# Two accumulator tiles for the last output strip of the first block's layers, and the squares of x on ScalarE

## The chip, the core and the metric

The kernel runs on one core of one Trainium2 chip. The core has TensorE (PE, with a weight load PEld ahead of each matmul), VectorE (DVE), ScalarE (ACT), GpSimd (POOL) and SyncE (SP), whose queue issues nearly all of the weight transfers here. The metric is the device time of one execution in microseconds (us).

## What is computed

A first block of two layers and a second block of one layer work on 256 tokens of width 2048. What matters here is how a layer of the first block ends and what follows it:

```python
# first block, layer l = 0, 1
mixed = jnp.concatenate([a_out, b_out, c_out], axis=-1)     # 256 x 2048
x = x + jnp.einsum('bsm,md->bsd', mixed, w_out[l])
# next layer, or the end of the block: x * rsqrt(mean(x*x) + EPS) * g
# second block
mod = silu(c) @ w_ada + b_ada          # six rows of 2048, and two more from w_ada_final
h = rms_norm(x, g_mix) * (1 + sc1) + sh1
...                                    # two attentions, output projection, residual
h = rms_norm(x, g_ffn) * (1 + sc2) + sh2
y = hier_moe(h)                        # router, then 32 experts
```

All of it is float32; a product with a weight is made of three matmuls on high and low parts.

## The kernel before

**Projections.** `proj` loads a weight strip of 512 columns in chunks of four blocks of 128 rows (`q`, 1 MB each, line 133). Each chunk is split in two halves (`hf`) into a high and a low part: ScalarE casts (L266), VectorE subtracts (L267), into one of three buffers `hl`. A half gives 12 matmuls in the token-major form (L295): two row blocks, two token halves `tb`, three products. With `by_op` false the 12 follow their half. With `by_op=True` the last chunk, and with `by_op="all"` every chunk, waits for both halves and then does the 12 matmuls of token half 0 and after them the 12 of token half 1.

**Accumulators.** `accum()` takes one of two PSUM tiles (pool `pa`, each of two banks, one for each token half). `Halves` takes both: one tile for each token half. It stands in the kernel before too, for the last strip of the second block's second output projection.

**End of a layer.** `layer` runs `part` for output strips 0 to 3 and `fin` after each. `fin` adds each token half of the accumulator to `x` (L919) and sums its squares (L920, by `square`: ScalarE at L378, VectorE at L380). In layer 1 it also multiplies x by the final gain (L922), sums the squares once more (L923) and, after the last strip, a chain of small operations (L953 to L961) leads by a power on GpSimd to the factor that the second block's first matmuls need.

**The modulation rows and the credit.** The eight rows `mod` (order 1, 0, 2, 4, 3, 5, 7, 6) are not made on TensorE. `ada_gen` makes them on VectorE in 256 steps: each takes one 512 KB load `araw` (three buffers, issued on SP's queue, L554) and one multiply-add over 128x1024 (L572; the first two of a row are L570). After 32 steps four small products on TensorE (`adap`, L578) sum a row up, and only then is the one buffer `ada` free for the next row. The steps are strewn among other work by a credit: `tick()` adds 0.590 after each half of a chunk, and a whole credit emits one step. `proj` doesn't call `tick` for a chunk that goes by `by_op`. What has not been emitted when the second block's last output strip begins is emitted there at once, by `ada_finish()` ahead of that strip's `proj`.

**Order.** The program gives each operation its place by a list scheduler: it goes by the order in which the operations are emitted and fills gaps that it foresees with later ones; each engine and SP's queue then run their list in order. `high_priority` around `fin` moves its operations ahead.

After the second block's output projection come the router (L1253 and on, many small VectorE operations), the gather (L1384) and the experts, whose weights (`ew`) go into buffers as these come free, those of `araw`, `ada`, `raw` and `hl` among them.

Of the kernel before, what the change touches and what calls it, by code (L numbers as in the profile page):

```python
# [94 lines left out]
def tile_kernel(tc, a, out, dbg=None):  # L95
    nc = tc.nc
    es = ExitStack()
    V = nc.vector
    A = nc.scalar
# [27 lines left out]
    def uid(s):  # L127
        cnt[0] += 1
        return f"{s}{cnt[0]}"
# [150 lines left out]
    def nb_ops(c, m):  # L280

        return [("N", c, m, tb, 0, tb) for tb in range(2)]
# [15 lines left out]
    def accum(name=None):  # L298
        return pa.tile([P, 2, 512], F32, tag="acc", name=name or uid("acc"))
# [74 lines left out]
    def square(xs, acc, eng):  # L374

        j = wk.tile([P, 512], F32, tag="stage", bufs=3, name=uid("sq"))
        if eng is A:
            A.activation(j, xs, AF.Square, accum_out=acc)  # L378
        else:
            V.scalar_tensor_tensor(j, xs, 1.0, xs, op0=OP.mult, op1=OP.mult, accum_out=acc)  # L380
# [90 lines left out]
    def mtile(name):  # L471
        return big.tile([P, 2, 4, S], F32R, tag="xm", bufs=7, name=name)
# [4 lines left out]
    ssq = sm.tile([P, 2, 4], F32, tag="ssq", name="ssq0")  # L477
# [132 lines left out]
    def layer(l, xT, ssq):  # L610
        w_in = a["w_in"][l]
        mT = [mtile(uid("mT")) for _ in range(4)]
# [47 lines left out]
        acc = latent(3078, 4, False)  # L660
# [3 lines left out]
        acc, started = accum(), set()  # L664
# [120 lines left out]
        acc = proj(w_in, 1536, 512, xT, nb_ops(0, 512))  # L785
# [3 lines left out]
        acc = proj(w_in, 2048, 262, xT, nb_ops(0, 262))  # L789
# [49 lines left out]
        for g in range(2):  # L839
            t = pslot([P, 4, S], F32, uid("cqk"))  # L840
            acc = proj(w_in, 4678 + 512 * g, 512, xT, tb_ops(4))
# [5 lines left out]
        acc = proj(w_in, 5702, 512, xT, nb_ops(0, 512))  # L847
# [8 lines left out]
        acc = proj(w_in, 6214, 512, xT, nb_ops(0, 512))  # L856
# [10 lines left out]
        for h in range(4):  # L867
# [19 lines left out]
            ssq = small(2, uid("css"))  # L887
# [15 lines left out]
        ssq = sm.tile([P, 2, 4], F32, tag="ssq", name=uid("ssq"))  # L903
        nxT = []
        accs = {}
        started = {s: set() for s in range(4)}

        def part(s, qs):
            accs[s] = proj(a["w_out"][l], 512 * s, 512, mT, nb_ops(0, 512), qs=qs, acc=accs.get(s), started=started[s],
                           final=qs[-1] == 3, by_op=True)  # L910

        def fin(s):
            if l == 1:
                gf = wk.tile([P, 512], F32, tag="stage", bufs=3, name=uid("gf"))
                nc.sync.dma_start(gf, a["final_norm_g"][512 * s : 512 * s + 512].unsqueeze(0).to_broadcast([P, 512]))
            with tc.high_priority():
                for tb in range(2):
                    xs = x[:, tb, 512 * s : 512 * s + 512]
                    V.tensor_add(xs, accs[s][:, tb, :], xs)  # L919
                    square(xs, ssq[:, tb, s : s + 1], V if l == 1 and s == 3 and tb else A)  # L920
                    if l == 1:
                        V.tensor_mul(xs, xs, gf)  # L922
                        square(xs, ssq1[:, tb, s : s + 1], V if tb else A)  # L923
            if l == 0:
                nxT.append(transpose_strip(s, "norm_g", 16))
# [14 lines left out]
    for l in range(DEPTH):  # L940
        xT, ssq, ssq1 = layer(l, xT, ssq)
# [154 lines left out]
    for u in range(2):  # L1096
# [5 lines left out]
        acc = proj(w_in, 3584 + 512 * u, 512, hT, nb_ops(0, 512))  # L1102
# [7 lines left out]
    for gp in range(2):  # L1110
        mT2.append(mtile(uid("oT")))
        qa = projT(512 * gp, "qa", qsplit)
        if gp == 0:
            ka = pslot([P, 4, S], F32, "ka")
            va = ka[:, 2:4, :]
            acc = proj(w_in, 1024, 512, hT, tb_ops(2) + [("N", 256, 256, 1, 0, 0), ("N", 256, 256, 1, 256, 1)])
# [100 lines left out]
    for s in range(4):  # L1217
        if s == 3:
            ada_finish()
        add_half(s, proj(a["w_out_2"][0], 512 * s, 512, mT2, nb_ops(0, 512), qs=(0, 1), by_op="all" if s == 3 else False,  # L1220
                         acc=Halves() if s == 3 else None), ra)
# [316 lines left out]
    for c0, n in STRIPS:  # L1538
# [8 lines left out]
        for v in range(4):  # L1547
            s, o = (c0 + m * v) // 512, (c0 + m * v) % 512
            h = slice(CAP * v, CAP * v + CAP)
            V.tensor_mul(yv(i, s)[P - CAP : P, o : o + m], ps[h, :], gt2(s)[h, o : o + m])  # L1550
        for s in range(c0 // 512, (c0 + n) // 512):
            xs = [x[:, tb, 512 * s : 512 * s + 512] for tb in range(2)]
# [11 lines left out]
    for s in range(4):  # L1564
        c = slice(512 * s, 512 * s + 512)
        for tb in range(2):
            xs = x[:, tb, c]
# [32 lines left out]
```

## Time and profile before

| | us |
|---|---|
| median of 3 runs | 2367.68 |
| lowest, highest | 2366.15, 2375.21 |
| profiled execution, device time | 2365.31 |
| its span, first to last instruction | 2363.6 |

TensorE is busy for 89% of the span, VectorE for 53%, ScalarE for 34%. The page cuts the span into 40 slices of 59 us. In the first 23 TensorE is busy for 80% or more nearly everywhere; from about 1390 us on, the transfers of the expert weights fill the 16 DMA engines at about 420 GB/s. Rows of the timeline give start, duration, engine, line, operation, what is written and read, the count, and in brackets the idle time of the engine ahead of it with what ended it. Rows that the profiler merged cover several instructions.

### The profile page before, as it was taken

The numbers are of one execution on the slowest core, as the hardware profiler recorded it, in microseconds if no ns is written. First come the engines' busy times: TensorE is split into PE (matmuls) and PEld (weight loads), VectorE is DVE, ScalarE is ACT, GpSimd is POOL, SyncE is SP. The second block draws the span as 40 slices with busy tenths as digits, with TensorE's granted clock in tenths as the row PEclk, the third lists the DMA queues.
The fourth block names the chain that finished last, engine by engine and source line by source line (L and its number), as shares of the span: only waits on it lengthen the run. The fifth ranks groups of instructions, "written<-read, shape, count | busy, mean of one in ns | idle before, by whom it ended". The sixth has DMA issues, their size and how long they took to land.

```text
span 2363.6 us, 32559 instructions
## 1 busy us (share of the span) xinstructions
PE 2108.8 (89%) x12919; PEld 1507.8 (64%) x12919; DVE 1253.7 (53%) x1990; ACT 793.6 (34%) x1583; POOL 100.0 (4%) x149
## 2 busy tenths in 40 slices
PE   8999999999999999899999988878777869696975
PEld 8999997799899977798786774333232424241421
DVE  5787687787776877775866871103021212121323
ACT  5553545545535555545555421100000101010111
POOL 0000100000100000202001000000000000000000
PEclk9999999999999999999999989989888989998998
DMA  6688787686797986796856899999999999999996
GB/s 212 219 298 286 240 313 268 235 306 205 242 311 249 317 287 231 231 339 185 308 187 237 291 356 376 421 421 421 421 419 421 421 421 421 421 421 421 421 421 253
DMA packets 221032, 760.82 MB, mean 322 GB/s; under 512 B 22464, under 2 KB 43276, under 8 KB 172616
## 3 DMA queue, kind: packets, MB, share of 16 engines
q1 hardware_dynamic: 215720, 750.88, 84.0%
q0 software_dynamic: 4960, 7.71, 1.5%
q8 instruction: 103, 1.69, 0.3%
q14 instruction: 57, 0.47, 0.1%
q10 hardware_dynamic: 192, 0.08, 0.0%
HBM read 755.68 MB, written 2.97 MB: 321 GB/s over the span
## 4 chain that ended last, share of the span: by engine, by line
PE 54%; DMA 26%; issue 11%; DVE 7%; ACT 2%; POOL 0%; SPq 0%; DVEq 0%; POOLq 0%; ACTq 0%
PE acc L291 19%; PE acc L295 16%; DMA ew<-in_w_up_dram 13%; DMA ew<-in_w_down_dram 6%; PE xg L1384 5%; DMA araw<-in_w_ada_dram 4%; PE acc L1428 2%; DVE ada L572 2%; PE gu L1406 2%; DVE hl L267 2%; PE s L431 2%; DMA araw<-in_w_ada_final_dram 2%; PE guT L1414 1%; PE pT L460 1%; PE op L1032 1%
## 5 line engine op out<-in xcount | busy, mean ns | idle before, releaser
L266 ACT CAST hl<-raw 128x1024 fp32r<-128x1024 f32 (+4 forms) x478 | 423.9, 897 | 493.6 <-PE acc L291 250.4
L267 DVE TENSOR_TENSOR hl<-raw,hl 128x1024 fp32r<-128x1024 f32 (+4 forms) x478 | 488.4, 1034 | 151.3 <-ACT hl L266 150.6
L291 PE MATMUL acc<-xT,hl 128*128 128x256 f32 x3744 | 469.5, 285 | 6.3 <-DVE hl L267 3.3
L291 PEld LDWEIGHTS acc<-xT,hl 128*128 128x128 f32 x3744 | 455.8, 192 | 12.1 <-ACT hl L266 5.2
L572 DVE SCALAR_TENSOR_TENSOR ada<-araw,cact,ada 128x1024 f32<-128x1024 f32 x240 | 306.9, 1287 | 79.9 <-DMA araw<-in_w_ada_dram 60.8
L1406 PE MATMUL gu<-ew,xe 128*32 128x512 f32 x1528 | 241.9, 646 | 92.3 <-DMA ew<-in_w_up_dram 58.9
L1419 DVE SCALAR_TENSOR_TENSOR eth<-eth,guT 128x128 f32<-128x128 f32 x32 | 9.2, 288 | 440.6 <-ACT eth L1418 440.6
L1411 ACT COPY gus<-gu 128x512 f32<-128x512 f32 x32 | 18.8, 586 | 613.0 <-PE gu L1406 613.0
L1406 PEld LDWEIGHTS gu<-ew,xe 128*32 128x32 f32 x1528 | 51.9, 114 | 267.0 <-issue 101.0
L295 PE MATMUL acc<-hl,mT 128*128 128x512 f32 x768 | 188.2, 397 | 0.7 <-DVE hl L267 0.7
L1428 PE MATMUL acc<-ew,aT 128*32 128x512 f32 x992 | 157.2, 760 | 26.9 <-DVE aT L1421 22.2
L291 PE MATMUL acc<-hT,hl 128*128 128x256 f32 x1248 | 170.4, 291 | 3.6 <-DVE hl L267 3.6
L291 PEld LDWEIGHTS acc<-hT,hl 128*128 128x128 f32 x1248 | 157.6, 194 | 13.4 <-issue 9.3
L295 PEld LDWEIGHTS acc<-hl,mT 128*128 128x128 f32 x768 | 141.9, 189 | 33.2 <-issue 3.7
L295 PE MATMUL acc<-hl,xT 128*128 128x512 f32 (+1 forms) x768 | 155.5, 364 | 2.4 <-DVE hl L267 2.4
L295 PEld LDWEIGHTS acc<-hl,xT 128*128 128x128 f32 x768 | 131.3, 188 | 25.7 <-DVE hl L267 3.3
L1384 PEld LDWEIGHTS xg<-oh,xres 128*128 128x128 f32 x512 | 122.8, 328 | 36.7 <-issue 26.8
L1432 DVE TENSOR_TENSOR y<-acc,gt2A 32x512 f32<-32x512 f32 x93 | 63.6, 684 | 150.7 <-PE acc L1428 149.7
L1384 PE MATMUL xg<-oh,xres 128*128 128x128 f32 x512 | 131.4, 411 | 5.4 <-ACT C L1375 3.2
L1406 PE MATMUL gu<-ew,xet 128*32 128x512 f32 x504 | 89.2, 635 | 30.1 <-DMA ew<-in_w_up_dram 23.3
L295 PE MATMUL acc<-hl,oT 128*128 128x512 f32 x384 | 101.4, 412 | 0.2 <-DVE hl L267 0.2
L1428 PEld LDWEIGHTS acc<-ew,aT 128*32 128x32 f32 x992 | 31.5, 131 | 106.5 <-issue 60.5
(339 smaller groups left out, 2013.0 us busy)
## 6 DMA issues: line engine op xcount, KB each, us to landing
ew<-in_w_down_dram SPq DMA_DIRECT2D x128, 1024.0 KB, 19.8
ew<-in_w_up_dram SPq DMA_DIRECT2D x127, 1024.0 KB, 19.8
ew<-in_w_gate_dram SPq DMA_DIRECT2D x126, 1024.0 KB, 19.8
raw<-in_w_in_dram SPq DMA_DIRECT2D x124, 1024.0 KB, 6.8
araw<-in_w_ada_dram SPq DMA_DIRECT2D x192, 512.0 KB, 6.3
raw<-in_w_out_dram SPq DMA_DIRECT2D x48, 1024.0 KB, 6.4
araw<-in_w_ada_final_dram SPq DMA_DIRECT2D x64, 512.0 KB, 6.4
raw<-in_w_in_dram SPq DMA_DIRECT2D x16, 512.0 KB, 3.8
```

The source lines that it names most:

```text
L266: A.copy(dst_hi, src)
L267: V.tensor_sub(dst_lo, src, dst_hi)
L291: T.matmul(acc[:m, b, o : o + 256], w[:, u, c : c + m], xk[v], start=st, stop=last and j == 2, skip_group_check=True)
L295: T.matmul(acc[:, b, o : o + m], xk[v][:, P * tb : P * tb + P], w[:, u, c : c + m], start=st, stop=last and j == 2, skip_group_check=True)
L431: T.matmul(ps[:, c0 : c0 + n], q_(b), k_[:, 0:n], start=b + i == 0, stop=i == len(terms) - 1, skip_group_check=True)
L460: T.transpose(ps[:, P * i : P * i + P], t[:, P * i : P * i + P], ident)
L572: V.scalar_tensor_tensor(ah, raw, ck, ah, op0=OP.mult, op1=OP.add)
L1032: T.matmul(o[half, :S], vs[i][0], pTs[i][:, 0:256], start=True, stop=False, skip_group_check=True)
L1384: T.matmul(ps[:, m * j : m * j + m], quads(x[:, tb, :], k), oh[:, tb, :], start=j + tb == 0, stop=tb == 1, skip_group_check=True)
L1406: T.matmul(ps[c : c + CAP, :], xe(i, k + d)[:, CAP * b : CAP * b + CAP], gu(v, k + d), start=k == 0, stop=k == KT - 2, skip_group_check=True)
L1428: T.matmul(acc[CAP * s : CAP * s + CAP, 0, :], aT[:, f, :], wd(f, s), start=f == 0, stop=f == 3, skip_group_check=True)
L1432: V.tensor_mul(yv(i, s)[CAP * b : CAP * b + CAP, :], acc[h, 0, :], gt2(s)[h, :])
```

## The change

For strip 3 of both layers of the first block the accumulator is a `Halves`, and `by_op` is "all" in place of True. The square of x in layer 1, strip 3, token half 1 goes to ScalarE as the others do.

```diff
         def part(s, qs):
-            accs[s] = proj(a["w_out"][l], 512 * s, 512, mT, nb_ops(0, 512), qs=qs, acc=accs.get(s), started=started[s],
-                           final=qs[-1] == 3, by_op=True)
+            accs[s] = proj(a["w_out"][l], 512 * s, 512, mT, nb_ops(0, 512), qs=qs, acc=accs.get(s) or (Halves() if s == 3 else None),
+                           started=started[s], final=qs[-1] == 3, by_op="all" if s == 3 else True)
...
                     V.tensor_add(xs, accs[s][:, tb, :], xs)
-                    square(xs, ssq[:, tb, s : s + 1], V if l == 1 and s == 3 and tb else A)
+                    square(xs, ssq[:, tb, s : s + 1], A)
```

## Rows read from the trace of the kernel before

**Rows 1.** The page, 40 slices: busy tenths of TensorE and of the DMA engines.
```profile
PE   8999999999999999899999988878777869696975
DMA  6688787686797986796856899999999999999996
```
**Rows 2.** Chain of work that ended last, in time: start, us, what.
```profile
1381.01 5.98 DMA araw<-in_w_ada_final_dram
1387.08 1.28 DVE ada L572
1388.37 1.32 DVE u L1156 x2
...
1401.94 7.35 PE xg L1384 x32
```
**Rows 3.** Timeline of the end of layer 1, all engines.
```profile
947.81 1.28 DVE L919 TENSOR_TENSOR xres<-acc,xres 128x512 f32<-128x512 f32 x2
...
962.12 1.23 DVE L267 TENSOR_TENSOR hl<-raw,hl 128x1024 fp32r<-128x1024 f32 x1 [1.50 <-ACT hl L266]
...
969.19 1.04 ACT L266 CAST hl<-raw 128x1024 fp32r<-128x1024 f32 x1 [0.30 <-PE acc L295]
969.19 1.29 DVE L919 TENSOR_TENSOR xres<-acc,xres 128x512 f32<-128x512 f32 x2 [5.85 <-PE acc L295]
970.14 0.62 ACT L378 ACTIVATE sq<-xres 128x512 f32<-128x512 f32 x1
...
970.89 0.69 DVE L922 TENSOR_TENSOR xres<-xres,gf 128x512 f32<-128x512 f32 x1 [0.41 <-ACT sq L378]
...
973.02 0.69 DVE L380 SCALAR_TENSOR_TENSOR sq<-xres 128x512 f32<-128x512 f32 x1
...
974.09 0.16 DVE L958 SCALAR_TENSOR_TENSOR rr_t<-rr_s,rr_t 128x2 f32<-128x2 f32 x1
...
976.43 1.19 PE L366 MATMUL bc<-diag,ones 128*128 128x128 f32 x4 [7.28 <-DVE diag L365]
```
**Rows 4.** Timeline of TensorE at the end of layer 0.
```profile
493.39 1.95 PE L291 MATMUL acc<-xT,hl 128*128 128x256 f32 x15
```
**Rows 5.** Timeline of TensorE in the second block's last output strip.
```profile
1382.09 4.82 PE L295 MATMUL acc<-hl,oT 128*128 128x512 f32 x20
```
**Rows 6.** Line L572, the modulation steps: ns min/median/max, first and last start.
```profile
L572 DVE SCALAR_TENSOR_TENSOR ada<-araw,cact,ada x240: 1261/1280/2262, 110.9 to 1387.1; 128x1024 f32<-128x1024 f32 x120
```
**Rows 7.** Timeline of VectorE: the last modulation row's first steps and late ones.
```profile
1254.94 1.41 DVE L570 TENSOR_SCALAR ada<-araw,cact 128x1024 f32<-128x1024 f32 x2
...
1358.94 1.28 DVE L572 SCALAR_TENSOR_TENSOR ada<-araw,cact,ada 128x1024 f32<-128x1024 f32 x1
...
1366.33 3.67 DVE L572 SCALAR_TENSOR_TENSOR ada<-araw,cact,ada 128x1024 f32<-128x1024 f32 x3
...
1375.74 1.28 DVE L572 SCALAR_TENSOR_TENSOR ada<-araw,cact,ada 128x1024 f32<-128x1024 f32 x1
```
**Rows 8.** Stages: us, busy of PE, PEld, DVE, ACT, POOL (instructions), clock, DMA share, GB/s.
```profile
960.00:980.00 20.00, 12.28 (x55) 10.03 (x54) 11.47 (x24) 6.66 (x11) 5.59 (x8) 0.83 0.43 138
...
1280.00:1300.00 20.00, 20.00 (x83) 14.20 (x83) 15.48 (x32) 12.63 (x32) 1.47 (x2) 0.91 0.61 208
...
1360.00:1380.00 20.00, 20.00 (x109) 16.91 (x107) 19.05 (x27) 8.71 (x14) 0.00 (x0) 1.00 0.91 316
```
**Rows 9.** Timeline of SP's queue: issues of modulation and expert loads.
```profile
1377.05 4.29 SPq L554 DMA_DIRECT2D araw<-in_w_ada_final_dram  x3
...
1381.86 2.64 SPq L1173 DMA_DIRECT2D ew<-in_w_down_dram  x4
...
1411.20 0.33 SPq L1194 DMA_DIRECT2D ew<-in_w_up_dram  x1
```
**Rows 10.** DMA issues: queue, count, KB each, median us from issue to landing.
```profile
ew<-in_w_down_dram SPq DMA_DIRECT2D x128, 1024.0 KB, 19.8
...
araw<-in_w_ada_final_dram SPq DMA_DIRECT2D x64, 512.0 KB, 6.4
```

## The prediction

> **What bounds the kernel now.** I read the page's 40 slices first. Up to about 1390 us TensorE sets the pace; from there the expert weights keep the DMA engines full to the end [rows 1]. In that second part a delay is not won back: the loads stop when all buffers are full, and start again when the first expert's matmuls free them. So what counts is when TensorE finishes the first part, and what stands between its last product and the gather. I then read the timeline at the two places that the change touches, and the chain of waits and the queues at the end of the second block's output projection, because the change also moves credit there.
>
> At the end of layer 0 TensorE has no gap to win: it goes straight on with layer 1's first projection at 493.39 [rows 4]. At the end of layer 1 it waits. The last product ends at 969.16; both adds start behind it, at 969.19, although token half 0 was done 12 matmuls before. The chain of squares and gains runs until 974.25, the power and two small products follow, and TensorE has its next work at 976.43, after 7.28 us idle [rows 3]; the granted clock of this stage is 0.83 [rows 8].
>
> At the third place, the last modulation step stands on the chain that ended last: its load takes 5.98 us, the step starts at 1387.08, and the residual add of the last strip follows it at 1388.37 [rows 2]. That row has nothing to spare.
>
> **The change part by part.**
>
> *Two tiles, layer 1.* One strip is 96 matmuls; from the adds at 947.81 to those at 969.19 it takes 21.38 us, 0.223 us for each [rows 3]. Token half 0 is complete 12 x 0.223 = 2.67 us before the end, so its add (0.68), square, gain and second square fall beside token half 1's matmuls. Left behind the last product: one add, 969.19 to 969.87. The square on ScalarE waits for the cast that starts there at 969.19 and takes 1.04, so it starts at 970.23; from its start to the gain it took 970.89 - 970.14 = 0.75, giving 970.98; the gain 0.61 to the next start, giving 971.59; from the second square's start to the end of the small operations 974.25 - 973.02 = 1.23, giving 972.82. Against 974.25 that is **-1.4 us**. Without the cast in front it would be -1.8; if a further VectorE split (1.23 [rows 3]) lands in the chain, -0.2. TensorE's gap is still near 6 us, so I count nothing for the clock.
>
> *The square moved to ScalarE.* VectorE is rid of 0.69 [rows 3], but the gain overwrites x and must wait for the square. The sum above already has this wait; kept on VectorE, the step would have ended within 0.3 us of the same. It goes in at nothing of its own, bounds -0.7 to +0.8 (one such square either way).
>
> *Two tiles, layer 0.* Nothing to win [rows 4]: 0. Added waits: the two tiles are both there are. Token half 1's first matmul needs the tile of strip 2; its adds end 1.3 us behind strip 2's last product (947.81 to 949.09 [rows 3]), and 12 matmuls of token half 0, 2.67 us, stand ahead. The next projection needs tile 0, freed by the first add about 2 us before the strip ends. If one modulation step (1.28 [rows 6]) sits in front, both are still about even: 0, bound +1.3 for each of the four places.
>
> *Every chunk by token half.* A half's buffer is free after 18 of 24 matmuls, and the split into it is needed 12 matmuls, 2.67 us, later. The split costs 1.04 + 1.23 = 2.27 us [rows 3]. It fits by 0.4 us. The nearest rows are the same form in the second block: 20 matmuls in 4.82 us, 0.24 each, without a gap [rows 5]. I take +0.5 for the six chunk changes of both layers; ends 0 and +4 (half of them behind a step of 1.28).
>
> *The credit.* This is the part that the change does not name. With every chunk of strip 3 by token half, its 6 calls of `tick` go, in two layers 12 x 0.590 = 7.08 credits. Counting through the program, 246 steps are emitted before the flush at the second block's last strip, so 10 are flushed; after the change 238, so **18 are flushed**. In strip 3 itself the missing steps buy nothing, since TensorE has no gap there. All later row boundaries move too: the seventh row's sum, now emitted in the second to last attention projection, is emitted in the second block's first output strip; the eighth row, which now begins at 1254.94 [rows 7], can begin only behind it, some 5 to 27 us later.
>
> What do 8 more steps cost in the end? One step is 3.67 / 3 = 1.22 us of VectorE [rows 7]. From below: if they fill VectorE's idle time between 1280 and 1340 (4.5 of 20 us idle in the row shown [rows 8]), 0. From above: in the flush three buffers turn round in 9.4 us (1366.33 to 1375.74 [rows 7]), so 8 steps take 25 us if all stand ahead of the router. Between: VectorE is busy for 19.05 of 20 us in this stage [rows 8], so 8 steps are 9.8 us of work, of which some 2 us find idle time. I take **+8 us**: nearer to this row, since VectorE's small router operations can go into the steps' load waits, but a list in order also stalls when a load is later than its place foresaw.
>
> Moving the loads costs no bytes: 8 x 512 KB leave stages of layers 0 and 1 and come later, before the gather's release at about 1411 [rows 9]; they fill time in which the queue would otherwise stand still.
>
> **Sum.** -1.4 + 0 + 0.5 + 8 = **+7 us**. Made on the profiled execution it is 2365.3 + 7 = 2372.3; that execution lies 2.4 us below the median of the runs, which the change is measured against, so I put it at 2367.7 + 7 = 2374.7, rounded to **2374**.
>
> **The rivals.**
>
> *Rival 1, the steps catch up.* For it: with idle VectorE time from 1280 to 1340 a filling scheduler can bring 8 steps in. Against it: the eighth row starts later, and VectorE has least room just where the steps would pile up. Then only -1.4 and the 0.5 are left: 2366 to 2368.
>
> *Rival 2, the tail stalls the router.* The last loads are issued when their buffers come free, from about 1385 on, behind 4 MB of expert weights issued at 1381.86 on the same queue [rows 9]. Expert loads that stand in such a queue land after 19.8 us, modulation loads now after 6.4 [rows 10]; two rounds of three loads, each later by half of the difference or by all of it (6 to 13 us) and in VectorE's list ahead of router operations, make +12 to +26: 2380 to 2393. It decides once more than three steps are left when the last product ends.
>
> The Trainium skill, page "DMA: Bandwidth & Descriptors", section "Queues, rings and completion order", says that each DMA engine consumes the descriptors of a ring in order, and that SP has one ring on each engine. That speaks for rival 2: by it the loads behind those 4 MB wait for all of them. The landing times in the rows agree; no row shows a modulation load in that place.
>
> *Rival 3, the two tiles do nothing.* If the scheduler puts the first add behind the strip anyway, -1.4 falls away: 2376 with the rest as forecast.
>
> *Rival 4, a real gain.* More than 11.8 us would need most of a gap at every strip; the traces show 7.28 us in one place. 2354.
>
> **How the numbers follow.** 0.5%, 11.8 us, is about what a measurement of this kernel tells from no change: 2356 to 2379.5. The forecast (2369 to 2380) has 0.44, rival 1 0.20, rival 2 0.28, rival 3 0.05, rival 4 0.03. The forecast's upper edge and rival 2 beyond 2379.5 make slower 0.31, faster 0.03, same 0.66. The range runs from 2364, rival 1 with its best bound, to 2389, which leaves out rival 4 and the top of rival 2.
>
> **What would show it.** Right: at layer 1's end the first add starts about 2.7 us before the last product ends, and TensorE's idle time is near 6 us; fewer L572 steps in both strips 3; the eighth row's first step later than 1254.94; L572 steps behind 1388, among router operations, and a gather later than 1401.94. If the last step stays at about 1388, rival 1 is right; if router operations wait over 5 us on an `araw` load, rival 2. The prediction is wrong if TensorE shows gaps inside the two strips, or if the time falls by more than 2 us.

## The result and the profile after

| | kernel before | kernel after |
|---|---|---|
| median, us (four runs each) | 2366.91 | 2397.05 |
| lowest, highest | 2362.5, 2375.21 | 2387.26, 2401.64 |
| profiled execution, device time | 2365.31 | 2387.26 |
| its span | 2363.6 | 2385.6 |

The ratio of after to before is 1.0123, 95% interval 1.0100 to 1.0146: slower by 1.2%, some 30 us. The forecast was 2374 with a range up to 2389. The loss has the sign of the forecast and four times its size. The profiled execution of after is its fastest run, 22 us above that of before, so its trace shows about three quarters of the loss of the medians. One of the six runs of e8 below took 8565 us and is left out of its median and ratio.

The page's slices for TensorE and the DMA engines stand against [rows 1]:

```profile
PE   8999999999999999899899968969677968686985
DMA  6688796796696986796865888999999999999996
```

A slice is 59.6 us here. TensorE's 20th (1133 to 1193 us) has 8 in place of 9 and its 24th (1372 to 1431 us) 6 in place of 8; behind that the DMA engines are as full as they were. A slice is coarse: a stall of 15 us in the 22nd and 23rd doesn't show.

The end of layer 1, timeline of all engines (start, us, engine, line), against [rows 3]:

```profile
962.45 0.69 DVE L919 TENSOR_TENSOR xres<-acc,xres 128x512 f32<-128x512 f32 x1 [1.77 <-PE acc L295]
...
965.17 0.69 DVE L919 TENSOR_TENSOR xres<-acc,xres 128x512 f32<-128x512 f32 x1 [0.54 <-PE acc L295]
...
966.38 0.62 ACT L378 ACTIVATE sq<-xres 128x512 f32<-128x512 f32 x1
...
971.26 1.19 PE L366 MATMUL bc<-diag,ones 128*128 128x128 f32 x4 [6.13 <-DVE diag L365]
```

The change does what it says. The first add starts 2.7 us before the last product ends (965.13), one add is left behind it, the moved square runs on ScalarE at 966.38, and TensorE's gap is 6.13 us instead of 7.28.

To find the loss I cut the first part of each profile at three places: the small product `bc` at the end of layer 1, the end of the last output product of the second block, and the start of the gather. Behind the gather the profiles of this study take 959 to 966 us to their ends (961.9 before, 963.2 after).

| profile | `bc` starts | to the end of the last product | from there to the gather | last step's end less last product's |
|---|---|---|---|---|
| before | 976.4 | 411.9 | 13.4 | 0.0 |
| after | 971.3 | 426.2 | 25.0 | +10.7 |

Two losses, then: 14.3 us between the end of layer 1 and the last product, and 11.6 us between the last product and the gather. Against them stands a `bc` that comes 5.2 us earlier; profiles whose code is the same up to there differ by as much (971.3 to 981.4), so I give it no cause. 14.3 + 11.6 - 5.2 = 20.7 us at the gather. Each kernel has one profile, and the stretch itself varies: before and the three kernels below that are as fast (e1, e17, e19) take 405.9 to 411.9 us for it. TensorE's idle time in it is steadier, 9.8 to 10.8 us in these four. In after it is 23.0 us.

The first loss has two main places. One is in the middle of the second block's attention (timeline of after; queue, VectorE and TensorE):

```profile
1133.33 13.77 SPq L554 DMA_DIRECT2D araw<-in_w_ada_final_dram  x5
...
1143.39 1.28 DVE L572 SCALAR_TENSOR_TENSOR ada<-araw,cact,ada 128x1024 f32<-128x1024 f32 x1 [3.17 <-DMA araw<-in_w_ada_final_dram]
...
1148.01 0.62 PE L291 MATMUL acc<-hT,hl 128*128 128x256 f32 x3 [2.92 <-DVE hl L267]
...
1152.16 1.22 PE L431 MATMUL s<-kb,qb 64*128 64x128 f32 x5 [3.53 <-DVE t L1050]
```

VectorE waits 3.17 us for one modulation load, and the splits and the score operation behind that step in its order come late. TensorE waits for them, 2.92 + 3.53 = 6.45 us. I call this **stall A**. The other place is ahead of the first residual adds of the second block:

```profile
1229.71 1.28 DVE L572 SCALAR_TENSOR_TENSOR ada<-araw,cact,ada 128x1024 f32<-128x1024 f32 x1
...
1300.83 1.01 PE L1024 MATMUL os<-ones,sqa 128*128 128x1 f32 x4 [3.34 <-POOL sqa L1019]
...
1302.76 7.04 PE L1146 MATMUL psb<-kk,modc 128*128 128x36 f32 x32 [0.33 <-DVE modc L542]
...
1309.73 1.94 PE L578 MATMUL adap<-ada,ones 128*32 128x512 f32 x8
...
1311.73 0.75 DVE L570 TENSOR_SCALAR ada<-araw,cact 128x1024 f32<-128x1024 f32 x1 [1.71 <-PE adap L578]
1312.40 1.41 DVE L1156 SCALAR_TENSOR_TENSOR u<-acc,rstd,gtA 128x512 f32<-128x512 f32 x2
...
1313.86 4.47 PE L295 MATMUL acc<-hl,oT 128*128 128x512 f32 x12 [2.20 <-DVE u L1156]
```

Both accumulators are full of output products, and only the adds (`u`) free them. The adds come at 1312.40, behind the last attention's norm (`os`), the router's bias (`psb`) and the seventh modulation row's sum (`adap`), none of which they need. This is **stall B**. In the kernel before the adds stand behind that sum, which comes 57 us earlier there, and ahead of the rest (timeline of VectorE and TensorE):

```profile
1253.13 1.06 PE L578 MATMUL adap<-ada,ones 128*32 128x512 f32 x8
...
1284.93 0.75 DVE L1156 SCALAR_TENSOR_TENSOR u<-acc,rstd,gtA 128x512 f32<-128x512 f32 x1 [3.13 <-PE acc L295]
...
1324.14 3.65 PE L1146 MATMUL psb<-kk,modc 128*128 128x36 f32 x32
```

The price of B is the idle time, 3.34 + 0.33 + 2.20 = 5.9 us, and the slower products in it: the 32 of `psb` take 7.04 us against 3.65, since the granted clock from 1300 to 1320 is 0.57. That is 9.3 us.

A and B are waits of after alone, and before has waits of its own. Idle time of TensorE, after less before, in windows counted from `bc`: 1.1 us more in the first 130 us, 3.7 more in the next 70 (stall A; before waits 1.77 and 2.39 us there), 3.0 less in the next 110, 6.3 more in the next 50 (stall B), and 4.0 more behind that. With the 3.4 us of slower products these make 15.5, against the 14.3 measured.

The missing credit itself had been made up by then. The steps of the seven rows (L570 and L572 together) number 172 in before and 165 in after at 982 us, and 224, seven whole rows, in both at 1240. Stall A lies in the stage that makes them up; that the one causes the other is not shown. The windows of line L572 (length, busy time of VectorE with the count, granted clock, DMA share, GB/s), first before, then after:

```profile
982.00:1240.00 258.00, 64.35 (x50) 0.98 0.76 255
1240.00:1310.00 70.00, 12.82 (x10) 0.93 0.71 244
...
982.00:1240.00 258.00, 73.31 (x57) 0.98 0.80 271
1240.00:1310.00 70.00, 0.00 (x0) 0.93 0.54 196
```

In after the seventh row's last step ends at 1230.99, but its sum runs at 1309.73, and up to 1311.73 VectorE makes no step at all. In before the last step ends at 1201.29 and the sum runs at 1253.13. So the eighth row is late because of the place of that sum in the order, not because steps were still missing.

The second loss is the flush. The chain of after, in order of time (start, us, what), against [rows 2]:

```profile
1387.95 6.90 DMA araw<-in_w_ada_final_dram
1394.95 1.30 DVE ada L572
1396.26 4.41 DMA araw<-in_w_ada_final_dram
1400.76 1.30 DVE ada L572
1402.07 4.64 DMA araw<-in_w_ada_final_dram
1406.81 1.30 DVE ada L572
...
1422.64 7.35 PE xg L1384 x32
```

Loads and steps alternate. Nine steps start behind 1388 (in before none), and the gather comes at 1422.64 instead of 1401.94. I call this **the tail**. The queue, VectorE and TensorE in the timeline of after:

```profile
1387.95 14.45 SPq L554 DMA_DIRECT2D araw<-in_w_ada_final_dram  x7
...
1392.37 1.22 DVE L267 TENSOR_TENSOR hl<-raw,hl 128x1024 fp32r<-128x1024 f32 x1
...
1393.64 3.78 PE L295 MATMUL acc<-hl,oT 128*128 128x512 f32 x8 [3.84 <-DVE hl L267]
...
1402.45 1.50 SPq L1173 DMA_DIRECT2D ew<-in_w_down_dram  x3
...
1406.81 1.28 DVE L572 SCALAR_TENSOR_TENSOR ada<-araw,cact,ada 128x1024 f32<-128x1024 f32 x1 [1.95 <-DMA araw<-in_w_ada_final_dram]
1408.01 1.40 DVE L1156 SCALAR_TENSOR_TENSOR u<-acc,rstd,gtB 128x512 f32<-128x512 f32 x2
```

Seven modulation loads hold SP's queue for 14.45 us and the expert loads wait behind them, not the other way round. The flush reaches into the first stretch too: the last split of the last strip stands behind two of its steps, and TensorE waits 3.84 us for it.

In the program's own list for VectorE the same is seen without times: of the 256 steps, 250 stand ahead of the adds of strip 2 in before and 243 in after, so 6 and 13 steps stand between the last two strips' adds; ahead of the first add stand 232 and 225. A row has 32 steps, so step 224 ends the seventh row: in after this **row boundary** stands right at the first adds.

### The profile page after: what moved, and what is told of

Same layout as the page of the kernel before. It is cut to its first block, busy times and chain, and to the rows that moved or that the text cites. A ratio compares the mean times of both kernels' runs of the same rounds, so it can differ in the third digit from the quotient of the medians.

```text
span 2385.6 us, 32549 instructions
## 1 busy us (share of the span) xinstructions
PE 2113.3 (89%) x12919; PEld 1511.8 (63%) x12919; DVE 1255.1 (53%) x1988; ACT 794.1 (33%) x1585; POOL 96.9 (4%) x149
## 4 chain that ended last, share of the span: by engine, by line
PE 56%; DMA 25%; issue 11%; DVE 5%; ACT 2%; POOL 0%; SPq 0%; DVEq 0%; POOLq 0%; ACTq 0%
PE acc L291 22%; PE acc L295 17%; DMA ew<-in_w_up_dram 13%; DMA ew<-in_w_down_dram 7%; PE xg L1384 4%; DMA araw<-in_w_ada_dram 3%; PE gu L1406 2%; DMA araw<-in_w_ada_final_dram 2%; DVE ada L572 2%; PE acc L1428 2%; PE s L431 2%; DVE hl L267 1%; PE pT L460 1%; PE guT L1414 1%; PE op L1032 1%
## 5 line engine op out<-in xcount | busy, mean ns | idle before, releaser
L572 DVE SCALAR_TENSOR_TENSOR ada<-araw,cact,ada 128x1024 f32<-128x1024 f32 x240 | 306.3, 1283 | 69.3 <-DMA araw<-in_w_ada_dram 49.4
L1406 PE MATMUL gu<-ew,xet 128*32 128x512 f32 x504 | 91.5, 645 | 33.1 <-DMA ew<-in_w_up_dram 24.2
L1414 PEld LDWEIGHTS guT<-fold,gus 128*128 128x128 f32 x256 | 62.1, 327 | 55.3 <-ACT gus L1411 55.3
```

Of the source, the lines that this page charges most:

```text
L572: V.scalar_tensor_tensor(ah, raw, ck, ah, op0=OP.mult, op1=OP.add)
L1406: T.matmul(ps[c : c + CAP, :], xe(i, k + d)[:, CAP * b : CAP * b + CAP], gu(v, k + d), start=k == 0, stop=k == KT - 2, skip_group_check=True)
L1414: T.matmul(ps[:, 2 * CAP * f : 2 * CAP * f + 2 * CAP], quads(g, f), fold, start=f == 0, stop=True, skip_group_check=True)
```

## The experiments

Each ratio is against runs of the kernel before on the same chip at the same time. "To product" and "to gather" are the two stretches of the table above, in the profile of that kernel.

| kernel | median, us | before | ratio, 95% interval | to product | to gather |
|---|---|---|---|---|---|
| e1_ticks_kept | 2364.73 | 2365.82 | 0.9998 (0.9984, 1.0013) | 407.7 | 12.6 |
| e2_credit_only | 2396.01 | 2365.82 | 1.0128 (1.0107, 1.0149) | 428.3 | 25.9 |
| e4_flush_behind | 2399.55 | 2365.82 | 1.0139 (1.0118, 1.0161) | 423.5 | 33.1 |
| e7_eight_steps_out | 2383.22 | 2365.82 | 1.0063 (1.0043, 1.0083) | 425.8 | 11.9 |
| e8_credit_late | 2390.10 | 2365.14 | 1.0107 (1.0084, 1.0129) | 437.7 | 12.0 |
| e9_credit_before_a | 2384.37 | 2365.14 | 1.0075 (1.0054, 1.0097) | 432.3 | 11.1 |
| e10_rate_611 | 2379.81 | 2365.14 | 1.0062 (1.0041, 1.0083) | 406.8 | 12.1 |
| e11_rate_640 | 2365.68 | 2365.14 | 1.0005 (0.9991, 1.0019) | 404.4 | 12.1 |
| e6_half_dose | 2380.38 | 2366.25 | 1.0066 (1.0048, 1.0084) | 417.3 | 19.3 |
| e5_double_dose | 2391.49 | 2366.25 | 1.0110 (1.0090, 1.0129) | 403.3 | 46.5 |
| e13_before_strip3_110 | 2371.06 | 2366.25 | 1.0030 (1.0014, 1.0046) | 407.0 | 12.0 |
| e14_tiles_strip3_110 | 2369.11 | 2366.25 | 1.0011 (0.9997, 1.0025) | 411.9 | 12.4 |
| e15_row_other_buffer | 2386.04 | 2366.14 | 1.0085 (1.0068, 1.0101) | 430.4 | 12.8 |
| e17_before_other_buffer | 2364.52 | 2366.14 | 0.9993 (0.9981, 1.0005) | 405.9 | 13.6 |
| e19_ticks_kept_other_buffer | 2364.93 | 2366.14 | 0.9989 (0.9973, 1.0006) | 406.7 | 13.2 |
| e20_double_dose_other_buffer | 2387.99 | 2366.14 | 1.0093 (1.0074, 1.0112) | 405.6 | 41.3 |
| e21_row_result_other_buffer | 2392.73 | 2364.90 | 1.0109 (1.0086, 1.0132) | 418.0 | 34.8 |
| e23_that_and_steps_out | 2373.41 | 2364.90 | 1.0036 (1.0020, 1.0051) | 417.8 | 13.5 |

### Which part of the change it is

e1 is the change with the credit kept: `tick` is called in the branch that goes by token half.

```diff
             if by_op:
...
+                    if not last:
+                        tick()
```

> The changed kernel with the six credits of strip 3 put back in both layers: two tiles, every chunk by token half, all squares on ScalarE, but the same 246 steps emitted ahead of the flush as in the kernel before. Theory credit (the loss comes from the steps that move to the flush): the loss is gone, 2358 to 2366, 0 to 8 us under the kernel before, and 6 steps stand between the residual adds of the last two strips as before. Rival tiles (the loss comes from the two tiles or from chunks by token half): 2385 to 2400 stays.

e2 is the kernel before with only the credit taken away, in strip 3 of both layers.

```diff
-                tick()
+                if not quiet:
+                    tick()
...
-                           final=qs[-1] == 3, by_op=True)
+                           final=qs[-1] == 3, by_op=True, quiet=s == 3)
```

> The kernel before with nothing changed but the credit: strip 3 of both layers no longer calls for a step after its halves; one tile, squares as before. Theory credit: 13 steps stand between the last two residual adds of the second block instead of 6, and the time rises by 20 to 35 us to 2387 to 2402. Rival tiles: 2365 to 2370, no change.

e2 loses 30 us, as much as the whole change, and its two stretches are those of after. e1 loses nothing that can be measured. So the credit is all of the loss, and the two tiles with the moved square are worth nothing that can be measured. In e1 too TensorE's gap at the end of layer 1 is 6.13 us, but in layer 0, where in before only one wait of 0.56 us stands, there are now four (timeline of TensorE, e1):

```profile
470.77 0.44 PE L396 MATMUL xt<-ident,xres 128*128 128x128 f32 x2 [1.28 <-DVE xres L921]
...
494.53 0.44 PE L396 MATMUL xt<-ident,xres 128*128 128x128 f32 x2 [1.33 <-DVE xres L921]
```

With 0.38 and 0.70 us at 483.83 and 497.46 that is 3.7 us. A step ends just where the add starts in both places (470.03 and 493.79 on VectorE). In after TensorE waits nowhere from 465 to 500, although more steps stand in that strip (seven L572 between the adds, in before five): none of them ends just where an add starts.

### Does the flush do it, and does credit elsewhere win it back?

e7 is after without the last eight steps, so what stays is what they do not cause.

```diff
-            for k in range(KT):
+            for k in range(KT if v != 6 else KT - 4):
```

> The changed kernel without the last 8 steps of the last modulation row (that part of the row's sum is left out; the loads are left out with them); 5 steps stand between the last two adds instead of 13. Theory credit with the price of a buffer round trip, some 2.4 us a step: 17 to 22 us under the changed kernel, near the kernel before or some us under it. If a step costs only VectorE's 1.2 us: 10 us under the changed kernel. Rival tiles: at most 3 us under it.

The stretch to the gather is back at 11.9 us, so the tail is gone, and 17 us of loss stay, in the stretch to the last product, where stalls A and B stand as in after. It is 14 us under after, between the two prices of the expectation.

e4 moves `ada_finish()` in after behind the last residual add, so that the router's operations needn't wait for the steps.

```diff
-        if s == 3:
-            ada_finish()
         add_half(s, proj(a["w_out_2"][0], 512 * s, 512, mT2, nb_ops(0, 512), qs=(0, 1), by_op="all" if s == 3 else False,
                          acc=Halves() if s == 3 else None), ra)
+        if s == 3:
+            ada_finish()
```

> The changed kernel with the flush emitted behind the last residual add instead of ahead of the last strip's projection; 3 steps then stand between the last two adds, 10 behind. Theory credit, by place in VectorE's list: the router starts about as early as before, and the loss falls to under 10 us (2360 to 2376). Rival load queue (the steps' loads stand behind expert weights and stall the router operations that follow them in the list): 2380 to 2400 stays, and router operations wait for modulation loads of over 5 us.

It is no faster, and the test was not clean: TensorE's list has the row's sum ahead of the transposes that lead to the router, as in after, where TensorE waits 7.58 us for it. Here it stood and waited 18.20 us for the steps (timeline of TensorE, e4).

```profile
1412.99 1.92 PE L578 MATMUL adap<-ada,ones 128*32 128x512 f32 x4 [18.20 <-DVE ada L572]
```

e8 and e9 give the eight steps back in one burst, e8 between the two halves of the second block's output projections, e9 ahead of its second attention; e10 and e11 raise the rate of all ticks (the diffs in this order; e11 has 0.640).

```diff
+    for _ in range(8):
+        next(ada_it, None)
     wtags = ["xm"] * 5 + ["hl", "ada", "hl", "hl"]
```

```diff
+    for _ in range(8):
+        next(ada_it, None)
     rb_ = out_rstd(sqb)
```

```diff
-    RATE = 0.590
+    RATE = 0.611
```

> The changed kernel with the 8 missing steps emitted at once between the two halves of the second block's output projection. The flush is as short as before the change (8 steps between the last two residual adds in place of 13), but the eighth row still begins as late as in the changed kernel, behind the first output strip. It parts the two places of the loss. If all of it is the flush: within 5 us of the kernel before, 2362 to 2371. If part of it is the late row boundary, where TensorE stood still around 1300 us: that part stays, 2370 to 2380. If the steps merely stall somewhere else: 2385 or more.

> The changed kernel with the 8 missing steps emitted at once earlier, between the two attentions of the second block, so that the eighth row begins ahead of the output projection as in the kernel before. Theory credit, both places: the loss is gone, 2358 to 2368; what is under 2365 is what the two tiles and the emptier strips 3 give. If the row boundary plays no part, the same time as with the steps emitted late.

> The changed kernel with the credit for a half chunk raised from 0.590 to 0.611, so that 344 halves give the 7 credits that the twelve silent ones no longer give; the list has the same number of steps ahead of each residual add of the second block as before the change. Theory credit: 2356 to 2366. Since the steps are spread over the other strips and strips 3 stay empty of them, up to 5 us under the kernel before. Rival tiles: 2385 or more.

> The changed kernel with the credit raised to 0.640, so that nothing is left to flush: all 256 steps stand ahead of the second strip of the last product. If the flush of 6 steps in the kernel before still costs time at the router, some 3 to 6 us under the same kernel at 0.611. If earlier stages have no room for the steps, the time is equal or up to 5 us more.

My expectation that giving the credit back would give the time back fell in e8, e9 and e10. All four lose the tail (to gather 11 to 12 us), but e8 and e9 take 26 and 20 us longer than before for the stretch to the last product. Stall A stands in both profiles and stall B in e8, so what the burst of steps costs by itself is not shown. e10 pays ahead of it: its `bc` starts at 993.9, 17.4 us behind that of before, more than profiles of equal code differ by. e11 ends level with before: its `bc` is 9.1 us late and the stretch to the last product, with few steps left in it, 7.5 us shorter. More steps early are not free either.

### How much per step

e6 takes away the credit of layer 1's strip 3 alone (8 steps between the last adds on the list), e5 that of strips 2 and 3 of both layers (`quiet=s >= 2`, 20 steps).

```diff
-                           final=qs[-1] == 3, by_op=True)
+                           final=qs[-1] == 3, by_op=True, quiet=s == 3 and l == 1)
```

> The kernel before without the credit of layer 1's strip 3 alone (layer 0's strip 3 keeps it): 4 credits missing instead of 8; 8 steps stand between the last two residual adds on the list (before 6, after 13), and the last row's boundary stays where it is in before's list or just past it. Theory 'price per step in the second block, 2 to 4 us': +8 to +16, 2374 to 2382. Rival 'the late row boundary is a threshold that costs 15 or more by itself': either +2 to +5 (boundary not crossed) or +20 and more (crossed). The trace's first L570 of the last row (before 1254.94, after 1311.73) says which.

> The kernel before without credit in strips 2 and 3 of both layers: 14 credits missing; 20 steps stand between the last two residual adds on the list (after 13). The last row's boundary moves behind the first residual add as in after. Theory 'price per step in the second block, 2 to 4 us': +35 to +60, 2402 to 2427. Rival 'the boundary is most of the loss, and flushed steps cost little': +30 or less, under 2397.

The loss does not grow with the credit: 3.5 credits less cost 14 us (e6), 7.1 cost 30 (e2), and 14.2 cost 25 (e5). A price for each step, which e6 alone would fit, is therefore not the right picture. In e6 the eighth row starts at 1297.25, between before and after. In e5 stalls A and B are missing and the tail is three times as long (timeline of VectorE and TensorE, e5):

```profile
1305.16 0.75 DVE L1157 SCALAR_TENSOR_TENSOR u<-acc,rstd,gtA 128x512 f32<-128x512 f32 x1 [0.79 <-PE acc L295]
...
1315.67 3.66 PE L1147 MATMUL psb<-kk,modc 128*128 128x36 f32 x32
...
1404.85 1.92 PE L579 MATMUL adap<-ada,ones 128*32 128x512 f32 x4 [27.54 <-DVE ada L573]
```

The adds stand ahead of `psb` again, since the row boundary now comes behind them in the program's list, and the stretch to the last product is even 8.6 us shorter than in before. Then TensorE waits 27.54 us for the steps.

e13 and e14 are the other direction: in strip 3 a tick is worth 1.100, in the kernel before (e13) and in the change with the ticks kept (e14), so that nothing is left to flush.

```diff
-                           final=qs[-1] == 3, by_op=True)
+                           final=qs[-1] == 3, by_op=True, rate=1.100 if s == 3 else RATE)
```

> The kernel before, with the credit of a tick raised from 0.590 to 1.100 in output strip 3 of both layers of the first block, so that the last row's steps run out before the second block's last strip and nothing is left to flush (before: 6 steps stand between the last two strips' residual adds on the list). Theory 'a step is priced by its place' (nearly free beside TensorE in strips 3, 2 us or more in the second block): the flush's steps go where they are hidden, so 8 to 14 us below before: 2351 to 2358. Rival 'a step costs the same everywhere' or 'more credit early shifts the whole list': nothing gained, 2362 to 2370, as with the higher rate everywhere. In the trace by the theory: no L572 behind about 1360, gather some 8 to 14 us earlier than 1401.74, and the end of layer 1 no later than 976 plus the 2 us that profiles of the same code differ by there.

> The kernel after, with a tick kept behind each half of a chunk in strip 3 at 1.100 credits: two tiles, all squares on ScalarE, and no step left to flush. Theory 'priced by place': as the kernel before with the same credit, give or take 2 us, 2351 to 2358. Rival 'the same everywhere': 2362 to 2370. If the tiles add VectorE collisions with 12 more steps in the strips that are cut by token half, up to 5 us more than the other kernel of this credit.

The theory that steps are nearly free in strips 3 fell: neither is faster, and e13 is 0.3% slower, clear of its interval (its profile is its fastest run and doesn't show where). Without any flush the stretch to the gather is 12.0 and 12.4 us, against 13.4 in before. So the flush of before costs some 1 us there. Its last step ends with its last product (1388.36 and 1388.32): before sits just where the flush begins to matter, and there was nothing to win.

### What holds the steps back

The eight rows share one buffer for their sums, and a row's result `arow` takes one of the three small buffers that the adds' `u` use too. e15 gives the eighth row's sum a buffer of its own, in after; e17 does so in before, e19 in the change with the ticks kept, e20 in e5.

```diff
-            acc = wk.tile([P, D], F32, tag="ada", bufs=1, name=uid("ada"))
+            acc = wk.tile([P, D], F32, tag="ada", bufs=1, name=uid("ada")) if v != 6 else big.tile([P, D], F32, tag="xm", bufs=7, name=uid("ada"))
```

> The kernel after, with the last row's sum in a buffer of its own (one of the seven of the activations, free by then), so that its first steps need not wait for the seventh row's products; the credit is as low as in after. On the list the steps then catch up: 236 stand ahead of the second block's first residual add (after 225, before 232), and 6 between the last two strips (after 13, before 6). Theory 'the one buffer holds the last row back': both parts of the loss go, 2362 to 2370, with TensorE's stall at 1297 to 1314 gone and the gather back to 1396 to 1404. Rival 'the missing credit itself costs, wherever the row begins': at most the stall goes, 2380 to 2388. Rival 'the buffer taken delays expert loads': the rest behind the gather grows by 3 us or more over the 955 us that it took in all runs.

> The kernel before with the last row's sum in a buffer of its own. On the list 238 steps stand ahead of the first residual add and 2 between the last two strips (before 232 and 6). The kernel before has no stall at its row boundary, and its last step ends with its last product (both at 1388.3), so by the theory there is little to win: 2361 to 2367. Rival 'steps between the last strips cost 2 us each': 8 us less, 2357 to 2360. If the buffer has a cost in expert loads, it shows here: 2370 and more.

> The kernel after with the ticks of strip 3 kept, and the last row's sum in a buffer of its own: two tiles without any loss of credit, 2 steps between the last two strips. By the theory the same as the kernel before with that buffer, less the 1.15 us that TensorE's gap at the end of layer 1 shrank by, plus the waits in layer 0's strip 3: within 2 us of it. If the tiles do gain, 2 to 4 us below it.

> The kernel before without the credit of strips 2 and 3, with the last row's sum in a buffer of its own. Here the list keeps the row boundary behind the first adds in either case, and 18 steps (20 without the buffer) stand between the last two strips. Theory 'the one buffer matters only where its wait stands ahead of the adds, and the flush costs what it adds behind the last product': 2384 to 2392, from last product to gather 40 us or more. Rival 'the buffer as such makes the loss': 2370 or less.

e15 met neither: its time lies in the range of the first rival, but the tail is what went (12.8) and the stalls are what stayed; the loss is 20 us (timeline of VectorE and TensorE, e15).

```profile
1276.85 0.75 DVE L570 TENSOR_SCALAR ada<-araw,cact 128x1024 f32<-128x1024 f32 x1
...
1323.60 1.94 PE L578 MATMUL adap<-ada,ones 128*32 128x512 f32 x8
1326.47 3.70 PE L295 MATMUL acc<-hl,oT 128*128 128x512 f32 x9 [0.93 <-DVE u L1156]
```

The eighth row starts at 1276.85, 47 us ahead of the seventh row's sum. So the one sum buffer is what makes the tail of after: while it is shared, the eighth row can't start before that sum. But the adds still come behind the sum, so this buffer isn't what holds them. e17 and e19 show that the buffer taken costs nothing that can be measured. In e20, which has 7 credits less than after, the list leaves 18 steps for the end in spite of the free buffer, and the tail stays: the buffer helps where the steps are there to be moved up. None of e15, e17 and e19 is measurably faster than before, nor is any other kernel here.

e21 gives `arow` of the seventh row another buffer, in after; e23 does the same without the last eight steps, as in e7.

```diff
-            row = wk.tile([P, 512], F32, tag="stage", bufs=3, name=uid("arow"))
+            row = wk.tile([P, 512], F32, tag="stage", bufs=3, name=uid("arow")) if v != 7 else big.tile([P, D], F32, tag="xm", bufs=7, name=uid("arow"))[:, 0:512]
```

> The kernel after, with the seventh row's result in a buffer of the activations in place of one of the three small buffers that it shares with the first residual adds. On the list the adds of strips 0 and 1 now stand ahead of the last attention's small products, and 14 steps stand between the last two strips (after 13). Theory 'the shared small buffer makes the stall': no stall at 1297 to 1314, 403 to 412 us from the end of layer 1 to the last product (after 426). The seventh row's products still come at about 1315, and the eighth row took 85 to 100 us from there in the runs that began it so late, so the last step ends at 1400 to 1415 and the loss does not all go: 2376 to 2392, with 25 us or more from last product to gather. Rival 'the stall has another cause': 420 us or more to the last product, 2390 to 2400.

> The same with the last eight steps of the last row left out (the last four of the sixteen row blocks of its sum, so the eighth modulation row is incomplete). Theory 'two parts, the stall and the row that ends late, and nothing else': both gone, 403 to 412 us to the last product and about 12 to 16 us from there to the gather, so 2360 to 2370, though the credit is as low as in after. Rival 'the missing credit costs in other places too': 2375 or more.

In e21 the adds are back in their place, and stall B is gone (timeline of VectorE and TensorE, e21):

```profile
1286.50 0.75 DVE L1156 SCALAR_TENSOR_TENSOR u<-acc,rstd,gtA 128x512 f32<-128x512 f32 x1 [0.39 <-PE acc L295]
...
1312.44 4.90 PE L1146 MATMUL psb<-kk,modc 128*128 128x36 f32 x32
1317.27 1.94 PE L578 MATMUL adap<-ada,ones 128*32 128x512 f32 x8
1319.27 1.42 DVE L570 TENSOR_SCALAR ada<-araw,cact 128x1024 f32<-128x1024 f32 x2 [1.71 <-PE adap L578]
...
1414.40 1.40 DVE L1156 SCALAR_TENSOR_TENSOR u<-acc,rstd,gtB 128x512 f32<-128x512 f32 x2
```

From 1285 to 1325 TensorE has no wait, and the stretch to the last product falls from 426.2 to 418.0 us. Next to nothing of it arrives: the loss is 28 us still, just above the range that I had expected. The eighth row starts at 1319.27, its last step ends at 1414.48, and the stretch to the gather grows from 25.0 to 34.8 us. The 8.2 us are given back as 9.8. With the last eight steps left out as well (e23) both are gone, and 8.5 us of loss stay. The stretch of 417.8 us is 5.9 us longer than that of before, TensorE's idle time in it is 17.4 us instead of 10.8, and the longest waits name a place (timeline of TensorE, e23):

```profile
1154.52 0.62 PE L291 MATMUL acc<-hT,hl 128*128 128x256 f32 x3 [2.69 <-DVE hl L267]
1158.67 2.08 PE L431 MATMUL s<-kb,qb 64*128 64x128 f32 x8 [3.53 <-DVE t L1050]
```

That is stall A, 6.2 us. It is not shown to be the whole rest: in the windows used above the idle time is 3.9 us more than in before around A, 3.0 less in the 110 us behind it, and 5.1 more in the last 58 us. I had expected A to be gone with the others, so the expectation for e23 (2360 to 2370) missed it; in e21 the same miss made 418 out of 403 to 412. By the medians, against before: without B and the tail 8.5 us (e23); with B 17.4 (e7); with the tail 27.8 (e21); with both 30.1 (after). So B costs 6 us by the ratios and 9 by the medians where the row's end doesn't set the time, and 2 to 3 us, which the intervals can't tell from nothing, where it does.

**What is shown and what stays open.** Shown: the credit alone is the loss (e1, e2); without the last eight steps the tail goes (e7), and 8.5 us stay when B is gone too (e23); the sum buffer makes the tail of after (e15), the small buffer of `arow` makes stall B (e21). Argued only: that A makes most of those 8.5 us, which no run took away by itself, and that the seventh row's sum stands behind the last attention because its PSUM buffer is one of two that the attention's products take in turn, in the order in which the program emits them. Open: why the modulation load ahead of 1143 is late in after and not in before. SP's queue has five such loads in a row over 13.77 us there, but no run moved them alone.

## Why the prediction was wrong

**What bounds the kernel** held. Behind the gather nothing is won back or lost, and the three places that were read are right. A fourth was not read: the second block's attention and the first adds behind it, where most of the 14.3 us that the first stretch lost lie. The windows of [rows 8] were read there as a measure of VectorE's room only.

**Two tiles, layer 1**: -1.4 was forecast and the gap shrank by 1.15 [rows 3]. The mechanism was right and the size nearly so. In the time it can't be seen (e1).

**The square at nothing, layer 0 at 0, every chunk by token half at +0.5**: held within what the runs can tell. After shows no wait of TensorE in layer 0's strip 3; the bound of +1.3 for each place was needed where a step ended just as an add could start (e1, 1.28 and 1.33).

**The credit, +8**: this is the step that failed. It priced the flush and left out what late steps and a late row sum do to TensorE ahead of it.

- *"The eighth row ... can begin only behind it, some 5 to 27 us later."* It began at 1311.73 instead of 1254.94, 57 us later [rows 7]. I placed the seventh row's sum where it is emitted. It ran behind the last attention, 79 us after the row's last step.
- *The bound of 25 us* priced the flush alone, and at 11.6 us that price was in the bounds, above the +8 taken. Its 9.4 us were no turn of the buffers: between 1366.33 and 1375.74 VectorE did splits and adds, and the step at 1375.74 waited for no load [rows 7]. In the flush of after three steps take 6.4 us. No part of the sum priced steps that delay TensorE elsewhere. That term, put at 0 by leaving it out, measured 14.3 us: late steps held splits back (A, and the wait of 3.84 us in the last strip), and a row boundary shifted up to the first adds held the accumulators (B). I had named the shift of "all later row boundaries", but followed only who starts later because of it, not who is queued behind.
- *"If they fill VectorE's idle time between 1280 and 1340"*, the lower bound. VectorE had idle time there, 9.44 of 20 us from 1280 to 1300 and 10.97 from 1300 to 1320 in after, yet no step ran before 1311.73: the only sum buffer was taken.

**Rival 1** (the steps catch up) is half right: the steps had caught up by 1240 us, and the eighth row then waited for the sum buffer. With that buffer free the tail is gone (e15). **Rival 2** forecast +12 to +26 with modulation loads late behind expert loads. Its price is the nearest, though the time lies above its 2393; its mechanism is not what happened: router operations wait for no load, the steps stand ahead of them, and the modulation loads hold the queue while the expert loads wait; their median from issue to landing is 5.5 us in after and was 6.4 in before. The Trainium skill (page "DMA: Bandwidth & Descriptors", section "Queues, rings and completion order") says that a ring's descriptors are consumed in order. Nothing here speaks against that; I had the two kinds of loads in the wrong order, and the issues at 1387.95 and 1402.45 show the right one.

**The signs** that were named came true but one: the add 2.7 us early, the gap near 6 us, the late eighth row, nine steps behind 1388, a later gather. Fewer steps in both strips 3 there are not: in layer 0's seven L572 against five in before, in layer 1's none in either. What they didn't cover is where TensorE would stand.

## What to carry to other kernels

A change to how one strip's products are ordered can also change how often a helper beside it is called. Count those calls first, and follow what they feed to where it becomes due, with every buffer that the late work holds or waits for, and with who is queued behind it on each engine. Work strewn among other work had no price per piece here: it cost little until a row, a buffer or the end of the other engine's work was reached, and then it cost in jumps; a kernel whose two chains end at the same time has no slack for either. Before removing one of two stalls, ask which limit stands behind it: stall B was worth 6 to 9 us with the row's end out of the way and next to nothing with it.

## What the runs showed of the chip that I had not expected

The same 32 small products (`psb`) took 3.65 us in before, 7.04 in after and 4.90 in e21. In after TensorE had little to do ahead of them and waited 3.34 us just before. The window of 1300 to 1320 us of after (its length, busy time of PE, PEld, DVE, ACT and POOL with their instructions, granted clock, DMA share, GB/s):

```profile
1300.00:1320.00 20.00, 16.64 (x68) 13.51 (x69) 9.03 (x16) 1.64 (x2) 4.66 (x6) 0.57 0.27 74
```

In the window of `psb` alone the granted clock is 0.50 in after, the lower of its two levels (1.2 of 2.4 GHz), 0.72 in e21 and 1.00, the upper level, in before. Time multiplied by granted clock gives 3.5 to 3.7 us in all three, so the stall cost 3.4 us more than its idle time. And a step of 1.28 us costs 2.1 us in the flush: the nine steps from 1388.90 to 1408.09 take 19.2 us, since loads of 4.41 to 6.90 us stand between them on the chain.
